# The second layer of a two-layer encoder rebuilt from half-size products in passes, with attention head by head

## The chip, the core and the metric

The kernel runs on one core of a Trainium2 chip, as one program. The metric is device microseconds from start to end; the median of three runs of the kernel before is 2737.35 us (2737.0 to 2742.38). All data is float32. Engines are named as in the profile: PE (TensorE, matmul), DVE (VectorE), ACT (ScalarE), POOL (GpSimd), and SP, the queue from which all of this kernel's transfers are issued, one after the other in the order of the program.

## The reference

2048 frames of 1024 channels go through two layers. The first is a gated mixer with its own projections; it is not changed. The second projects a shared K and V, a Q and a gate z, attends over a band of the own and eight previous chunks of 64 frames with a bias by relative position, gates, and projects out:

```python
k, v = jnp.split(rms_norm(x, g_kv) @ w_kv, 2, axis=-1)
...
q, z = jnp.split(h @ w_qz, 2, axis=-1)
...
sc = jnp.einsum('bqhd,bkhd->bhqk', qc, kc).astype(jnp.float32) + bias
sc = jnp.where(valid[None, None, None, :], sc, NEG_INF)
p = jax.nn.softmax(sc, axis=-1).astype(vc.dtype)
return jnp.einsum('bhqk,bkhd->bqhd', p, vc)
...
return (o * jax.nn.silu(z)) @ w_out
```

There are 16 heads of 64 channels. Five products of 2048 x 1024 by 1024 x 1024 make the dense work of this layer: V, K, Q, z and the output. The sum with x and a last RMS norm follow.

## The kernel before

Every float32 operand of a product is split into a high part, rounded to a format that TensorE multiplies at its full rate, and the low rest. Three matmuls (high by high, high by low, low by high; `mm3`, lines 95 to 98) stand for one. ACT writes the high part and DVE the low one.

The first layer does its six projections and its output by one level of Strassen's recursion: a product of two matrices, each cut into two by two quarters, is made of seven products of quarters (phases 1, 2, 6, 5, 7, 4, 3) in place of eight. A *pass* is one such product of 2048 x 1024 by 1024 x 1024: seven phases of eight steps, each step one PSUM tile of 128 x 512 with 12 matmuls. `run_steps` writes them in order, with operands prepared three steps ahead (`LOOK`). The left operand's combinations are split once and kept in DRAM (`hsd`, tile S); the right operand's are made from the raw weights by POOL, ACT and DVE (`make_t`, tile T).

The second layer (from 1401 us on, lines 938 ff.) does without the recursion. It goes over four blocks of 512 frames (t) and, within each, over eight pairs of heads (p). `project` makes V, Q and K of the next pair and `gate` its z (`one`, tiles pj and vp: 24 matmuls of 512 columns for a pair's K, Q or z, 24 of 256 columns for each 128 frames of V) while `score`, `flip` and `value` do the attention of the present pair. A `score` is 128 queries by up to 640 keys (tile s) with the softmax after it on DVE, ACT, DVE and POOL (lines 1062 to 1073). A `flip` transposes the probabilities on PE (tile tp, line 1093) and splits them. A `value` (tile pv, lines 1113 to 1120) multiplies two query blocks' probabilities by V. K and V of the block before come back from DRAM (`khd`, `vhd`), the scaled weights too (`wk3`, `wvv`). `share` and `take` say how many pieces of projection stand between two pieces of attention. `b4` is the output product of a block (tile bo), after the block's last head. A gain-scaled weight is loaded, multiplied on POOL and stored (`load_scaled`, lines 161 to 168) the first time.

The order of the instructions on each engine is written out by these loops; a layer below adds the semaphores, and each transfer on SP stands behind all earlier ones there.

## Time and profile before

One execution was profiled: 2736.74 us, span 2734.9 us.

| stretch (us) | what | PE busy | DVE busy | ACT busy | GB/s |
|---|---|---|---|---|---|
| 100 to 400 | first layer | 291 of 300 | 182 | 93 | 321 |
| 400 to 700 | first layer | 298 of 300 | 199 | 114 | 289 |
| 1070 to 1400 | its output product | 316 of 330 | 230 | 99 | 247 |
| 1400 to 1735 | second layer, first block | 326 of 335 | 225 | 177 | 205 |
| 1735 to 2660 | second layer, the other blocks | 922 of 925 | 731 | 561 | 150 |
| 2660 to 2735 | last block's output, end | 61 of 75 | 56 | 30 | 64 |

Matmuls overlap, so the duration of one (0.39 us for 512 columns) is longer than the distance between two starts; busy time is the time in which at least one runs. The transfer share of a window is the mean busy share of the 16 transfer engines, and a packet counts as busy from its start to its end, also while it waits.

### The profile page before, as it was taken

What the parts mean: (1) busy time and instruction counts of PE and PEld (TensorE: products, weight loads), DVE (VectorE), ACT (ScalarE), POOL (GpSimd) and SP (SyncE); (2) the same over time, 40 slices, a digit from 0 to 9 for tenths busy, and PEclk for the clock granted to TensorE, in tenths of its full rate; (3) what the DMA queues carried; (4) which work ended last, traced back from release to release, by engine and by line L of the source; (5) the groups of instructions that cost most, each with busy time, mean ns of one, the idle gap of its engine ahead of it and who ended that gap; (6) DMA issues with size and microseconds to landing.
All of it is one profiled execution on the core that took longest, in us unless ns stands there. A gap on an engine that the chain in (4) does not pass through costs nothing.

```text
span 2734.9 us, 39924 instructions
## 1 busy us (share of the span) xinstructions
PE 2667.4 (98%) x14176; PEld 2265.3 (83%) x14176; DVE 1926.6 (70%) x3211; ACT 1275.3 (47%) x2244; POOL 710.0 (26%) x767
## 2 busy tenths in 40 slices
PE   8899999999999999999999999999999999999997
PEld 6788888888778788777877888899988999889996
DVE  5655566756667667666766666877778777787777
ACT  5423243443433434222235554566655666556663
POOL 3511123241231422722024430211212212021111
PEclk9999999999999999999999999999999999999998
DMA  7799998986877869768767655545455455454432
GB/s 277 275 326 328 324 329 310 318 307 235 309 260 245 319 218 319 264 209 292 260 215 240 203 194 168 165 151 152 151 174 167 147 154 151 150 163 118 116 111 69
DMA packets 209190, 607.16 MB, mean 222 GB/s; under 512 B 24288, under 2 KB 24288, under 8 KB 208992
## 3 DMA queue, kind: packets, MB, share of 16 engines
q1 hardware_dynamic: 208992, 604.62, 66.0%
q8 instruction: 113, 1.85, 0.3%
q14 instruction: 85, 0.70, 0.1%
HBM read 466.11 MB, written 127.93 MB: 217 GB/s over the span
## 4 chain that ended last, share of the span: by engine, by line
PE 43%; DVE 7%; DMA 6%; POOL 2%; issue 1%; ACT 1%; SPq 0%; DVEq 0%; POOLq 0%; ACTq 0%
PE pj L96 5%; PE pj L97 5%; PE pj L98 5%; PE s L1054 4%; PE tp L1093 4%; PE pv L1120 4%; PE vp L98 2%; PE vp L96 2%; PE vp L97 2%; PE bo L96 2%; PE bo L98 2%; PE bo L97 2%; DMA xr<-in_x 2%; DMA A<-ytd 1%; DMA bx_b<-x1d 1%
## 5 line engine op out<-in xcount | busy, mean ns | idle before, releaser
L96 PE MATMUL P<-T,S 128*128 128x512 f32 x1248 | 496.0, 397 | 3.3 <-ACT S L255 2.1
L98 PE MATMUL P<-T,S 128*128 128x512 f32 x1248 | 490.4, 393 | 0.0
L97 PE MATMUL P<-T,S 128*128 128x512 f32 x1248 | 488.9, 392 | 0.6 <-DVE T L258 0.6
L1073 POOL TENSOR_SCALAR pr<-pr,sl 128x640 f32<-128x640 f32 (+4 forms) x256 | 198.7, 777 | 748.1 <-DVE sl L1072 662.1
L1069 ACT ACTIVATE pr<-pr,nm 128x640 f32<-128x640 f32 (+4 forms) x256 | 195.6, 764 | 270.2 <-DVE nm L1062 264.9
L96 PE MATMUL pj<-hh_b,wh_b 128*128 128x512 f32 x768 | 311.4, 406 | 0.7 <-ACT hh_b L150 0.7
L97 PE MATMUL pj<-hl_b,wh_b 128*128 128x512 f32 x768 | 302.3, 394 | 0.0
L98 PE MATMUL pj<-hh_b,wl_b 128*128 128x512 f32 x768 | 301.2, 392 | 0.0
L98 PEld LDWEIGHTS P<-T,S 128*128 128x128 f32 x1248 | 235.2, 188 | 50.0
L96 PEld LDWEIGHTS P<-T,S 128*128 128x128 f32 x1248 | 235.3, 189 | 45.7 <-ACT S L255 2.3
L97 PEld LDWEIGHTS P<-T,S 128*128 128x128 f32 x1248 | 235.6, 189 | 43.6 <-DVE T L258 1.0
L1097 DVE TENSOR_TENSOR pt<-tp,pt 128x640 fp32r<-128x640 f32 (+4 forms) x256 | 188.6, 737 | 60.2 <-ACT pt L1096 57.8
L1062 DVE CUSTOM_DVE_ANT_0 pr<-s,bias 128x640 f32<-128x640 f32 (+4 forms) x256 | 188.1, 735 | 48.7 <-PE s L1054 44.1
L98 PEld LDWEIGHTS pj<-hh_b,wl_b 128*128 128x128 f32 x768 | 144.2, 188 | 33.2
L1096 ACT CAST pt<-tp 128x640 fp32r<-128x640 f32 (+4 forms) x256 | 159.0, 621 | 22.9 <-PE tp L1093 17.8
L1093 PE MATMUL tp<-ident,pr 128*128 128x128 f32 x1120 | 164.8, 273 | 3.5 <-DVE pt L1097 2.0
L96 PEld LDWEIGHTS pj<-hh_b,wh_b 128*128 128x128 f32 x768 | 144.6, 188 | 19.6 <-ACT hh_b L150 0.9
L1093 PEld LDWEIGHTS tp<-ident,pr 128*128 128x128 f32 x1120 | 134.7, 140 | 31.4 <-issue 2.7
L97 PEld LDWEIGHTS pj<-hl_b,wh_b 128*128 128x128 f32 x768 | 145.0, 189 | 17.4
L96 PE MATMUL vp<-wh_bv,hh_b 128*128 128x256 f32 x512 | 148.3, 290 | 1.1 <-ACT hh_b L150 1.1
L98 PE MATMUL vp<-wh_bv,hl_b 128*128 128x256 f32 x512 | 145.6, 284 | 0.6 <-DVE hl_b L151 0.4
L97 PE MATMUL vp<-wl_bv,hh_b 128*128 128x256 f32 x512 | 145.1, 283 | 0.0
(216 smaller groups left out, 6054.9 us busy)
## 6 DMA issues: line engine op xcount, KB each, us to landing
S<-hsd SPq DMA_DIRECT2D x288, 512.0 KB, 5.0
rw<-in_w_a SPq DMA_DIRECT2D x108, 512.0 KB, 5.6
raw_b<-wk SPq DMA_DIRECT2D x75, 512.0 KB, 4.1
A<-ytd SPq DMA_DIRECT2D x72, 512.0 KB, 5.0
hsd<-S SPq DMA_DIRECT2D x56, 512.0 KB, 3.7
rwo<-in_w_out SPq DMA_DIRECT2D x40, 512.0 KB, 5.0
bias<-reld SPq DMA_DIRECT2D x64, 320.0 KB, 3.7
raw_bo<-in_wb_out SPq DMA_DIRECT2D x36, 512.0 KB, 3.8
```

The lines of the kernel that those rows point to most:

```text
L96: mm(ps, lh, rh, start=first, stop=False)
L97: mm(ps, lh, rl, start=False, stop=False)
L98: mm(ps, ll, rh, start=False, stop=last)
L1054: mm(ps[:, sg, :w], q[:, qb * P : (qb + 1) * P], kx[:, koff + sg * w : koff + (sg + 1) * w], start=i == 0, stop=i == 1,)
L1062: nc.vector.tensor_tensor_reduce(out=pr[:, c0:].rearrange("p (a b) -> p a b", a=nseg), in0=ps[:, :nseg, :w], in1=bias[:, c0:].rearrange("p ...
L1069: nc.scalar.activation(pr[:, c0:], pr[:, c0:], AF.Exp, scale=-1.0, bias=nm[:], accum_out=sl[:])
L1073: nc.gpsimd.tensor_scalar(pr[:, c0:], pr[:, c0:], sl[:], 1.0, op0=ALU.mult, op1=ALU.mult)
L1093: tpose(tp[:, b, :], pr[:, b * P : (b + 1) * P], ident[:])
L1096: nc.scalar.copy(oh, tp[:, b0:5, :])
L1097: nc.vector.tensor_tensor(pt[:, 1, b0 + qq : 5 + qq, cs], tp[:, b0:5, :], oh.bitcast(F32), op=ALU.subtract)
L1120: mm(po[:, 0, :], keys(i), pt[:, j, i, :], start=(t == 0 and j == 0 and i == blocks[0]), stop=(j == 1 and i == blocks[-1]),)
```

## The change

The first layer stays. The second layer's five products become passes of the recursion.

- V is a pass behind the first layer's output, on the same steps. The normalized rows are transposed and split as in the first layer's first pass, and each of the seven combinations of the rows goes to DRAM (`hs2`).
- K and Q of heads 0 to 7 are one pass behind it ("K"): the weights are now the stationary operand, and the rows' combinations come back from `hs2` in groups of four steps (`sg_load`, 2 MB each). K and Q are split and stored to DRAM (`kqd`). Beside this pass `prep_t` makes and stores the seven weight combinations of two further passes (`tbd`, 56 stores of 512 KB).
- Attention goes head by head over all 2048 frames: 256 blocks of `score` and `flip`, a `value` for each two. K, Q and V of a head are loaded from DRAM. Beside it run the two further passes (`dense`): n = 2 is K and Q of heads 8 to 15, n = 3 is z. Each is cut in two by columns, so there are four half passes, and each loads all of the rows' combinations: 56 units of 2 MB (`unit_load`), one ahead, into two buffers. `share` spreads 448 pieces of three matmuls over 250 blocks. Outputs, and z when ready, go to DRAM; `gate` loads both, multiplies on POOL and stores the product (`ogd`).
- The output is a last pass behind attention ("B"), with x added and the last norm as its steps end.

```diff
-        steps += [(n, ph, j) for n in (2, 3, 4, 5, "o") for ph in PH for j in range(NJ)]
+        steps += [(n, ph, j) for n in (2, 3, 4, 5, "o", "V", "K") for ph in PH for j in range(NJ)]
...
+        def prep_v(ph, j):
+            a11, a12 = va_[j][:, 0:512], va_[j][:, 512:1024]
+            if ph in (1, 6):
+                return s_split(ph, j, a11, "V")
+            if ph == 3:
+                tg(a12, a12, a11, op=sub)
+            if ph in (2, 3):
+                return s_split(ph, j, a12, "V")
+            return s_load(ph, j, "V")
...
+        def sg_load(ph, g):
+            i = len(sgs)
+            pool, tag, bufs = (kqp[0], "Sg", 2) if i % 3 else (sh, "hh", 1)
+            t = pool.tile([P, 4, 2, 4, P], F32R, tag=tag, name=f"Sg{i}", bufs=bufs)
+            nc.sync.dma_start(
+                t[:].rearrange("p j a k c -> p j a (k c)").bitcast(F32),
+                hs2[ph, g][:],
+            )
+            sgs[ph, g] = t
...
+        def product_k(ps, t, w):
+            o = ps[:].rearrange("p (a b) -> p a b", a=4)
+            for k in range(4):
+                mm3(o, w[k][0], w[k][1], t[:, :, 0, k, :], t[:, :, 1, k, :], k == 0, k == 3)
...
+            def put(ph, v):
+                hi, lo = (
+                    ca.tile([P, 1024], F32R, tag="S", name=f"wt{n}{q}_{ph}{i}", bufs=6)[:]
+                    for i in range(2)
+                )
+                split(hi, lo, v)
+                for i, t in enumerate((hi, lo)):
+                    nc.sync.dma_start(tbd[n, ph][:, i, q, :], t.bitcast(F32))
...
+        for u in range(4):
+            for i, f_ in enumerate(prep_t(2 + u // 2, u % 2)):
+                at(nk + 3 + 13 * u + 2 * i, f_)
...
+            def load_k(h):
+                t = kt[h] = sb.tile([P, S], F32R, tag="K", name=f"K{h}", bufs=2)
+                for i in range(2):
+                    nc.sync.dma_start(
+                        t[i * 64 : i * 64 + 64].bitcast(F32),
+                        kqd[0][h // 2][i, h % 2 * 64 : h % 2 * 64 + 64, :],
+                    )
...
+            units = [
+                (n, cq, ph, g) for n, cq in ((2, 0), (2, 1), (3, 0), (3, 1)) for ph in PH
+                for g in range(2)
+            ]
...
+            def unit_load(i):
+                if i >= len(units):
+                    return
+                n, cq, ph, g = units[i]
+                if g == 0:
+                    cs = slice(cq * 256, cq * 256 + 256)
+                    for hl in range(2):
+                        w = wq[n, cq, ph, hl] = sh.tile(
+                            [P, 2, 2, 256], F32R, tag="T", name=f"w{n}{cq}_{ph}_{hl}", bufs=8
                         )
+                        nc.sync.dma_start(
+                            w[:].bitcast(F32),
+                            tbd[n, ph][:, hl].rearrange("p q (k c) -> p q k c", k=2)[:, :, :, cs],
+                        )
+                t = sgq[i] = sh.tile(
+                    [P, 4, 2, 4, P], F32R, tag=("hl", "hh")[i % 2], name=f"Sq{i}"
+                )
+                nc.sync.dma_start(
+                    t[:].rearrange("p j a k c -> p j a (k c)").bitcast(F32), hs2[ph, g][:]
+                )
...
+            def dense():
+                base = 10000
+                unit_load(0)
+                for i, (n, cq, ph, g) in enumerate(units):
+                    unit_load(i + 1)
+                    for ct in range(2):
+                        flush(base + 2 * i + ct)
+                        ps = pmm.tile([P, 512], F32, tag="mm", name=f"Pb{n}{cq}_{ph}_{g}{ct}")
+                        o = ps[:].rearrange("p (a b) -> p a b", a=4)
+                        t = sgq[i]
+                        for k in range(4):
+                            w = [
+                                wq[n, cq, ph, hl][:, k // 2, k % 2, ct * P : ct * P + P]
+                                for hl in range(2)
+                            ]
+                            mm3(o, *w, t[:, :, 0, k, :], t[:, :, 1, k, :], k == 0, k == 3)
+                            yield
+                        evict(10 * n + cq, ph, 2 * g + ct, ps, done_b(n, cq))
+                flush(1 << 20)
...
+                first = max(0, 4 - 2 * g)
+                full = range(max(first, 1), 5)
+                seq = [(i, slice(0, 256)) for i in full]
+                if first == 0:
+                    seq.append((0, slice(0, P)))
+                seq.append((5, slice(P, 256)))
+                for n, (i, cs) in enumerate(seq):
+                    for j in range(2):
+                        mm(
+                            po[:, g % 2, cs], keys(i), pt[:, j, i, cs],
+                            start=g % 2 == 0 and n == 0 and j == 0,
+                            stop=g % 2 == 1 and n == len(seq) - 1 and j == 1,
                         )
...
+            def gate(p, t):
+                v = sh.tile([P, 2, 512], F32, tag="raw", name=f"og{p}_{t}", bufs=4)
+                cs = slice(t * 512, t * 512 + 512)
+                nc.sync.dma_start(v[:, 0], od[p][:, cs])
+                nc.sync.dma_start(v[:, 1], zd[p][:, cs])
+                nc.gpsimd.tensor_tensor(v[:, 0], v[:, 0], v[:, 1], op=ALU.mult)
+                nc.sync.dma_start(
+                    ogd[p // 4, t][:, :, p % 4, :], v[:, 0].rearrange("p (a b) -> p a b", a=4)
+                )
...
+            def one_gate():
+                for i, x_ in enumerate(gates):
+                    if x_ in zready:
+                        gate(*gates.pop(i))
+                        return
...
+            def share(b):
+                return 224 * min(1.0, (b + 1) / 116) + 224 * max(0.0, min(1.0, (b - 115) / 134))
...
+                if b + 2 < NB2:
+                    score(b + 2)
+                take(share(b - 0.5))
+                flip(b)
+                if b % 2 == 0 and b:
+                    value(b // 2 - 1)
+                take(share(b))
+                one_gate()
+            value(NB2 // 2 - 1)
...
+            steps = [("B", ph, j) for ph in PH for j in range(NJ)]
```

Three places show what moves. Names carry t, pair or head, and block; a name with w30 is the weight of the third pass's first half, Sq a group of rows.

PE beside attention, before (block 2, pair 5): six matmuls of a projection stand between a score and a flip.

```order
L1054 MATMUL s2_5_3_20479<-K2_2_1_19968,Qh2_2_1_19865 128x320 x2
L1054 MATMUL s2_5_3_20479<-K2_2_1_19968,Ql2_2_1_19866 128x320 x2
L96 MATMUL pj2_2_2_20442<-hh_b2_18434,wh_b2_2_2_20438 128x512
L97 MATMUL pj2_2_2_20442<-hl_b2_18435,wh_b2_2_2_20438 128x512
L98 MATMUL pj2_2_2_20442<-hh_b2_18434,wl_b2_2_2_20439 128x512
L96 MATMUL pj2_2_2_20442<-hh_b2_18434,wh_b2_2_2_20438 128x512
L97 MATMUL pj2_2_2_20442<-hl_b2_18435,wh_b2_2_2_20438 128x512
L98 MATMUL pj2_2_2_20442<-hh_b2_18434,wl_b2_2_2_20439 128x512
L1093 MATMUL tp2_5_1_20497<-ident_128,pr2_5_1_20387 128x128 x5
L96 MATMUL pj2_2_2_20442<-hh_b2_18434,wh_b2_2_2_20438 128x512
```

And after, in head 9:

```order
L1225 MATMUL tp9_3_20406<-ident_80,pr9_3_20343 128x128 x4
L84 MATMUL Pb30_5_01_20402<-Sq34_20158,w30_5_0_20154 128x512
L85 MATMUL Pb30_5_01_20402<-Sq34_20158,w30_5_0_20154 128x512
L86 MATMUL Pb30_5_01_20402<-Sq34_20158,w30_5_1_20156 128x512
L1188 MATMUL s9_6_20419<-K9_20007,Q9_1_20295 128x320 x4
L84 MATMUL Pb30_5_01_20402<-Sq34_20158,w30_5_0_20154 128x512
L85 MATMUL Pb30_5_01_20402<-Sq34_20158,w30_5_0_20154 128x512
L86 MATMUL Pb30_5_01_20402<-Sq34_20158,w30_5_1_20156 128x512
L1225 MATMUL tp9_4_20435<-ident_80,pr9_4_20366 128x128 x5
L1256 MATMUL pv9_0_20380<-pt9_2_20373,V4_0_19403 128x256 x6
L1256 MATMUL pv9_0_20380<-pt9_2_20373,V4_0_19403 128x128 x2
```

The pieces are of three matmuls now, with fewer of them per score, and the moving operand Sq and the weight w30 are both fresh from DRAM.

SP where K of a pair is projected, before:

```order
L995 DMA Qh2_2_0_19859<-Qh2_2_0_19859 64x512 [waits DMAHW2_49,Activation_49]
L995 DMA Ql2_2_0_19860<-Ql2_2_0_19860 64x512 [waits DMAHW3_49,DVE_49]
L995 DMA Qh2_2_1_19865<-Qh2_2_1_19865 64x512 [waits DMAHW4_49,Activation_49]
L161 DMA raw_b2_4_1_20620<-wk3_4_68 128x1024 [waits DMAHW5_49,DVE_49]
L995 DMA Ql2_2_1_19866<-Ql2_2_1_19866 64x512 [waits DMAHW6_49,DVE_49]
L1009 DMA K2_2_1_19968<-khd1_2_86 128x512 [waits DMAHW7_49]
L1007 DMA khd2_2_94<-K2_2_0_19963 128x512 [waits DMAHW0_49,DVE_49]
L1009 DMA K2_3_0_20426<-khd1_3_87 128x512 [waits DMAHW1_49,PE_49]
L161 DMA raw_b2_4_0_20721<-wk3_4_68 128x1024 [waits DMAHW2_49,DVE_49]
L1007 DMA khd2_2_94<-K2_2_1_19968 128x512 [waits DMAHW3_49,DVE_49]
```

And where K is a pass, after:

```order
L920 DMA Sg2_13610<-hs2_2_0_231 128x4096 [waits DMAHW3_49]
L203 DMA rwK_6_011_13638<-in_w_b 128x1024 [waits DMAHW4_49,DVE_49]
L203 DMA rwK_6_001_13640<-in_w_b 128x1024 [waits DMAHW5_49,DMAHW0_49,Pool_49]
L203 DMA rwK_6_111_13642<-in_w_b 128x1024 [waits DMAHW6_49,DMAHW1_49,Activation_49]
L990 DMA tbd2_1_291<-wt20_10_13644 128x1024 [waits DMAHW7_49,Activation_49]
L990 DMA tbd2_1_291<-wt20_11_13645 128x1024 [waits DVE_49]
L990 DMA tbd2_2_292<-wt20_20_13694 128x1024 [waits Activation_49]
L990 DMA tbd2_2_292<-wt20_21_13695 128x1024 [waits DMAHW2_49,DVE_49]
L990 DMA tbd2_3_293<-wt20_30_13700 128x1024 [waits DMAHW3_49,Activation_49]
L990 DMA tbd2_3_293<-wt20_31_13701 128x1024 [waits DMAHW4_49,DVE_49]
L951 DMA kd0_243<-kq0_0_0_13708 128x512 [waits DMAHW5_49,Activation_49]
L951 DMA kd0_243<-cK_0_13682 128x512 [waits DMAHW6_49,DVE_49]
```

In place of half a megabyte of weights, and K and V rows of 256 KB, stand groups of rows of 2 MB (Sg, shape 128x4096), raw weights and stores of weight combinations (tbd); each store waits for ACT or DVE.

SP beside attention, before, with the next pair's weights and the V of the block before:

```order
L1031 DMA bias2_5_20166<-reld5_117 128x640 [waits DMAHW4_49,DVE_49]
L967 DMA vhd2_1_109<-V2_1_0_20042 128x512 [waits DMAHW5_49,DVE_49]
L967 DMA vhd2_1_109<-V2_1_1_20093 128x512 [waits DMAHW6_49,DVE_49]
L967 DMA vhd2_1_109<-V2_1_2_20160 128x512 [waits DMAHW7_49,DVE_49]
L161 DMA raw_bv2_2_0_20831<-wvv2_74 128x1024 [waits DMAHW0_49,DVE_49]
L967 DMA vhd2_1_109<-V2_1_3_20215 128x512 [waits DMAHW1_49,DVE_49]
L975 DMA Vh2_2_0_20823<-vhd1_2_106 128x512 [waits DMAHW2_49,PE_49]
L975 DMA Vh2_2_1_20825<-vhd1_2_106 128x512 [waits DMAHW3_49,PE_49]
```

And after, where the first gate is made (og0):

```order
L1117 DMA w30_6_0_19781<-tbd3_6_303 128x4x256 [waits DMAHW5_49]
L1117 DMA w30_6_1_19783<-tbd3_6_303 128x4x256 [waits DMAHW6_49]
L1124 DMA Sq32_19785<-hs2_6_0_239 128x4096 [waits DMAHW7_49,PE_49]
L1146 DMA zd0_14893<-c30_0_19694 128x512 [waits DMAHW0_49]
L1281 DMA og0_0_19809<-od0_14885 128x512 [waits DMAHW1_49]
L1077 DMA Q8_2_19836<-qd4_255 64x2x512 [waits DMAHW2_49]
L1282 DMA og0_0_19809<-zd0_14893 128x512 [waits DMAHW3_49,DMAHW0_49]
L1077 DMA Q8_2_19836<-qd4_255 64x2x512 [waits DMAHW4_49]
L1084 DMA V4_2_19839<-vsd1_8_283 128x256 [waits DMAHW5_49]
L1084 DMA V4_2_19839<-vsd1_9_284 128x256 [waits DMAHW6_49]
L1284 DMA ogd0_0_14901<-og0_0_19809 512x1x128 [waits DMAHW7_49,Pool_49]
L1084 DMA V4_2_19839<-vsd1_10_285 128x256
```

The gate's two loads and its store stand with four other loads among them, and the store waits for POOL; the next group of rows (Sq32) and its weights stand ahead.

981 lines of the change are left out of this document (469 added, 512 removed).

## The prediction

> **What bounds the kernel now.** I read the busy shares and the 40 slices of the page first, then the window of the second layer, then the order in time of TensorE's work there, then the rows on transfers.
>
> ```profile
> PE 2667.4 (98%) x14176; PEld 2265.3 (83%) x14176; DVE 1926.6 (70%) x3211; ACT 1275.3 (47%) x2244; POOL 710.0 (26%) x767
> ...
> DMA  7799998986877869768767655545455455454432
> GB/s 277 275 326 328 324 329 310 318 307 235 309 260 245 319 218 319 264 209 292 260 215 240 203 194 168 165 151 152 151 174 167 147 154 151 150 163 118 116 111 69
> DMA packets 209190, 607.16 MB, mean 222 GB/s; under 512 B 24288, under 2 KB 24288, under 8 KB 208992
> ```
> ```profile
> 1401.00:2735.00 1334.00, 1307.87 (x7874) 1156.23 (x7872) 1011.41 (x2046) 767.41 (x1444) 302.01 (x471) 0.99 0.51 159
> ```
>
> TensorE is busy all the time. In the second layer (from 1401 us, the window row: length, busy time of PE, PEld, DVE, ACT, POOL, clock, DMA share, GB/s) it is busy for 1308 of 1334 us, while transfers run at 159 GB/s, half of what the first layer moves (the slices fall from 329 to about 150). So the second layer is bound by TensorE and has transfers to spare. The change trades one for the other.
>
> What one matmul costs is the distance between starts, since they overlap:
>
> ```profile
> 1703.11 0.39 PE L98 MATMUL bo<-wh_bo,ol 128*128 128x512 f32 x1
> ...
> 1705.38 0.39 PE L96 MATMUL bo<-wh_bo,oh 128*128 128x512 f32 x1
> ```
> ```profile
> 2002.26 0.46 PE L1054 MATMUL s<-K,Qh 128*128 128x320 f32 x2
> 2002.55 0.46 PE L1054 MATMUL s<-K,Ql 128*128 128x320 f32 x2
> 2002.85 0.28 PE L96 MATMUL vp<-wh_bv,hh_b 128*128 128x256 f32 x1
> ...
> 2003.08 0.28 PE L98 MATMUL vp<-wh_bv,hl_b 128*128 128x256 f32 x1
> 2003.20 0.28 PE L96 MATMUL vp<-wh_bv,hh_b 128*128 128x256 f32 x1
> ...
> 2003.56 0.40 PE L96 MATMUL pj<-hh_b,wh_b 128*128 128x512 f32 x1
> 2003.80 0.40 PE L97 MATMUL pj<-hl_b,wh_b 128*128 128x512 f32 x1
> 2004.03 0.39 PE L98 MATMUL pj<-hh_b,wl_b 128*128 128x512 f32 x1
> 2004.26 0.71 PE L1093 MATMUL tp<-ident,pr 128*128 128x128 f32 x5
> 2004.72 0.36 PE L1113 MATMUL pv<-pt,Vh 128*128 128x256 f32 x1
> ...
> 2006.00 0.40 PE L96 MATMUL pj<-hh_b,wh_b 128*128 128x512 f32 x1
> ```
>
> The ten intervals from 1703.11 to 1705.38 give 0.227 us for 512 columns, 0.23 between attention work. 256 columns take 0.12 us, one block's scores 0.59, its five flips 0.46, one pair's values 1.28. The count for the second layer before: pj 2304 x 0.23 = 530, vp 1536 x 0.12 = 184, bo 768 x 0.227 = 174, flips 1120 x 0.092 = 103, scores 192 x 0.59 and 64 of the first four blocks of a head at some 0.35 (by their columns) = 136, values 96 x 1.28 and 32 short ones at 0.7 (six matmuls) = 145, transposes 128 x 0.11 (eight in 0.87) = 14. Sum 1286 of 1334; 48 are waits, 18 of them the tail from the last matmul to 2734.9, as two rows of the chain that ended last show:
>
> ```profile
> 1393.88 0.87 PE tr_b L145 x8
> ...
> 2716.72 0.24 PE bo L98
> ```
>
> **What it takes from TensorE.** Seven products of half size replace eight. Dense work is then five passes (V; K and Q of half the heads; K and Q of the rest; gates; output) of 672 matmuls of 512 columns. Per stage: V 672 x 0.227 and 224 transposes x 0.11 = 177; K 152; attention with the two passes beside it 1344 x 0.23 = 309, flips 103, scores 136, values 149 (eight matmuls of 256 columns and four of 128 per pair; the narrow ones I put between 0.06 and 0.12 us, half and all of the 256-column price, so 1.2 to 1.44, taken 1.32); output 152. Sum 1179, so 107 us less.
>
> **What it adds in transfers.** Counted in units of 512 KB from the new code. V: weights 18, rows 16, the split rows stored 56 and read back 24, V out 32: 146. K: weights 18, 14 groups of split rows at 4 units = 56, weight combinations for the later passes 16 read and 56 stored, K and Q out 32: 178. Attention: split rows 56 x 4 = 224 (each of the four half passes reads all of them again), combined weights 56, K 32, Q 64, V 32, bias 10, outputs and gates to DRAM and back 80, K and Q of the second pass 32: 530. Output: 91. In all 945 units, 495 MB, against 159 GB/s x 1334 us = 212 MB before. The price of a unit is bounded by the fastest stretches of this trace:
>
> ```profile
> 450.00:460.00 10.00, 10.00 (x50) 7.99 (x49) 5.38 (x7) 2.95 (x5) 0.00 (x0) 1.00 1.03 416
> 360.00:400.00 40.00, 38.54 (x180) 31.45 (x179) 23.53 (x32) 17.66 (x28) 14.68 (x11) 1.00 0.96 348
> 440.00:500.00 60.00, 60.00 (x278) 48.96 (x277) 40.63 (x51) 19.23 (x31) 16.54 (x11) 1.00 0.97 332
> 450.00:550.00 100.00, 98.16 (x469) 80.11 (x468) 69.20 (x92) 38.55 (x61) 16.69 (x13) 1.00 0.96 326
> ```
>
> Over 10 us 416 GB/s (1.26 us a unit), over 40 us 348, over 100 us 326 (1.61). The long stretches are held back by demand too, TensorE being busy throughout, and the new stages queue more than the engines can take, so I go above the middle: 380 GB/s, 1.38 us a unit. Then V needs 201 us of transfers against 177 of TensorE, K 246 against 152, attention 731 against 697, output 126 against 152. Three of the four stages turn from TensorE to transfers, and K is the clearest: nothing there covers the 94 us, since each group of rows is loaded only three steps (2.7 us each) ahead, behind the stores of weights and results on the one queue.
>
> **The queue.** Each of 32 gates loads two tiles, multiplies on POOL and stores, in order on SP. The trace has that pattern in 32 scaled weights:
>
> ```profile
> SPq L168 <- DMA raw_b<-in_w_kqz: 44.7, 17, 4.0
> SPq L168 <- POOL raw_b L165: 40.5, 21, 3.0
> ...
> SPq L168 <- POOL raw_bv L165: 14.3, 7, 2.3
> SPq L168 <- DMA raw_bv<-in_w_vv: 7.5, 6, 2.9
> ```
>
> SP stood for 107 us on these, 3.3 a store. Hidden then, behind spare transfers; now it lies in the half of attention that needs most of them. Between nothing and 107; other loads stand between a gate's loads and its store, so I take 50.
>
> **The joins.** The output pass needs the last head's gated output, which goes through DRAM twice before the first product, and its weights queue behind that store:
>
> ```profile
> 2688.17 0.59 ACT ot L1132
> 2688.78 0.70 DVE ot L1134
> ```
> ```profile
> hsd<-S SPq DMA_DIRECT2D x56, 512.0 KB, 3.7
> ```
>
> Copy and add 1.3, store, load and store again with POOL between, then weights at 3.7 a transfer and their split: 18 us (10 to 25). V's start follows the first layer as the projections did; the tail after the last product stays 18.
>
> **Vector engines.** In attention VectorE has 256 blocks at 0.735 and 0.737 us, and some 220 us of reciprocals, evictions, splits and gates: about 600 of 697. No bound by itself.
>
> ```profile
> L1097 DVE TENSOR_TENSOR pt<-tp,pt 128x640 fp32r<-128x640 f32 (+4 forms) x256 | 188.6, 737 | 60.2 <-ACT pt L1096 57.8
> L1062 DVE CUSTOM_DVE_ANT_0 pr<-s,bias 128x640 f32<-128x640 f32 (+4 forms) x256 | 188.1, 735 | 48.7 <-PE s L1054 44.1
> ```
>
> **The sum.** V 201 + K 246 + attention 731 + 50 + output 152 with 2% of waits, 156 + join 18 + tail 18 = 1420, where 1334 stood. On the profiled span of 2734.9: 2821. That execution took 2736.7 us, 1.8 around the span, and the median of the runs shown, 2737.35, is 0.6 above it; with these 2.4 the forecast is 2824 us, 3% slower.
>
> **The rivals.** (a) Transfers keep up: 416 GB/s all the way, gates hidden. V 184, K 224, attention at TensorE's 697, output 156, 36 for join and tail: 1297, so 2700, faster. It decides at one number: the whole stands level at 1.28 us a unit with the 50 us of the gates (410 GB/s), at 1.34 without (392). Only 10 us stretches were that fast, but none had so deep a queue. (b) TensorE stays the bound, transfers hidden: 1179 + 30 of waits + 36 = 1245, so 2648. K would need 178 units in 152 us, 612 GB/s; no row comes near. (c) A cap: what the trace holds for 40 us, 348 GB/s, is all that the engines give in a stage that always has transfers queued, and the 10 us stretch was a burst. A unit is 1.507 us: V 220, K 268, attention 799 and 50, 156, 36: 1529, so 2932. For it speaks that the transfer share is 0.96 or 0.97 in all three long rows; against it that a share over 0.96 goes with 416 GB/s as well, so a long share may count packets that only wait. [...]
>
> **How the numbers follow.** The forecast (2745 to 2890) gets 0.52, (c) and what lies around it, 2890 to 3000, 0.23, beyond 0.03 (the gates' full 107 and a dry queue on top), (a) 0.15, (b) 0.03, level 0.04. A difference under 0.2% (5 us) can't be told from none here. That is 0.19 faster, 0.04 same, 0.77 slower. The range goes from (a)'s 2700 to 2960, (c) with half of the gates' other 57; what it leaves out, (b), all beyond 2960 and a little below 2700, is about 0.2.
>
> **What would show it.** Right: K takes about 246 us with a transfer share near 1 and TensorE waiting on loads of Sg at every fourth step; attention shows PE waiting on Sq, more in its second half; SP waits on POOL at the gate's store. Wrong: a rate of 400 GB/s or more held over hundreds of us, which brings (a). Waits over some 4 us could also halve the clock as here, where the matmuls behind an idle stretch take 0.43 us each; K at half clock would take 14 x 48 x 0.43 = 289.
>
> ```profile
> 1386.97 0.43 PE Po L96
> 1387.40 0.43 PE Po L97
> ```

## The result: 16% slower, and where the time went

The changed kernel takes 3176.25 us (median of four runs, 3165.43 to 3189.63), the kernel before 2737.18 beside it: 1.1605 times as long, with a 95% interval of 1.1556 to 1.1654. The forecast was 3% slower with a range that ended at 2960; the direction was right, the size far too small. The profiled execution took 3165.43 us with a span of 3163.6.

The page of the changed kernel, busy shares and the 40 slices:

```profile
PE 2766.8 (87%) x13216; PEld 2244.3 (71%) x13216; DVE 1865.8 (59%) x2973; ACT 1219.4 (39%) x2110; POOL 895.8 (28%) x807
...
PEclk9999999999999999989998879999999988798897
DMA  7898989777686976758899998888967888877864
GB/s 280 310 326 317 339 306 317 292 251 288 238 318 238 314 248 223 278 205 339 331 347 376 356 355 262 276 288 273 284 209 242 279 253 250 265 236 219 276 204 164
DMA packets 314834, 883.40 MB, mean 279 GB/s; under 512 B 32272, under 2 KB 93712, under 8 KB 303632
```

The second layer, stage by stage (length, busy time of PE, PEld, DVE, ACT, POOL, clock, DMA share, GB/s): V; K; attention with the side passes; join and output; tail.

```profile
1399.00:1610.00 211.00, 187.19 (x888) 150.98 (x888) 123.02 (x182) 85.07 (x143) 58.02 (x49) 0.96 0.86 322
1610.00:1874.00 264.00, 175.82 (x672) 138.52 (x672) 118.93 (x128) 104.83 (x145) 76.46 (x50) 0.84 0.96 360
1874.00:2933.00 1059.00, 874.47 (x4702) 713.03 (x4702) 541.21 (x1247) 447.52 (x911) 252.25 (x332) 0.90 0.83 258
2933.00:3147.00 214.00, 170.72 (x677) 133.54 (x675) 164.59 (x246) 53.59 (x79) 94.81 (x70) 0.90 0.67 220
3147.00:3163.00 16.00, 0.42 (x1) 0.00 (x0) 10.81 (x26) 0.00 (x0) 3.80 (x6) 0.61 0.44 164
```

| stage | forecast us | measured us |
|---|---|---|
| V | 201 | 211 |
| K, first to last product | 246 | 246 |
| last K product to first scores | none | 18 |
| attention, first scores to last values | 731 + 50 | 1059 |
| join | 18 | 16 |
| output products | 156 | 198 |
| tail | 18 | 16 |
| sum | 1420 | 1764 |

K came out to the microsecond, with a share of 0.96 and TensorE waiting for Sg as forecast (engine, line, releaser: us, times, longest):

```profile
PE Pk L84 <- DMA Sg<-hs: 74.6, 10, 13.0
```

Of the 344 us that are missing, attention has 278. TensorE is no longer full there (874 of 1059, the clock at 0.90 after 1.00 in the same stage before), and the transfers are not quite full either (0.83).

What ended TensorE's, the other engines' and SyncE's waits in attention (read as the line above):

```profile
ACT pt L1228 <- PE tp L1225: 263.2, 202, 7.7
DVE pt L1229 <- ACT pt L1228: 205.8, 180, 4.6
POOL og L1283 <- DMA og<-zd: 82.3, 22, 12.1
PE tp L1225 <- DVE pt L1229: 68.0, 76, 2.4
...
PE s L1188 <- DMA Q<-qd: 21.2, 5, 17.8
PE Pb L84 <- DMA Sq<-hs: 17.1, 4, 6.7
```
```profile
SPq L1269 <- DVE o L1268: 228.1, 30, 17.6
SPq L1284 <- POOL og L1283: 108.6, 29, 8.1
```

TensorE's longest waits in sum stand at the flips (68 us here for their buffer), not at Sq (17). A stretch of TensorE's work in order of time tells why: two flips of five blocks stand one behind the other, with nothing between them, and the first four blocks of the second wait 2.39 us for the one transpose buffer.

```profile
2102.25 0.39 PE L86 MATMUL Pb<-Sq,w 128*128 128x512 f32 x1
2102.48 0.72 PE L1225 MATMUL tp<-ident,pr 128*128 128x128 f32 x5
2105.58 0.63 PE L1225 MATMUL tp<-ident,pr 128*128 128x128 f32 x4 [2.39 <-DVE pt L1229]
2105.97 0.48 PE L84 MATMUL Pb<-Sq,w 128*128 128x512 f32 x1
```

The chain that ended last shows four in a row at another place (start, us, work), 2.5 us each where the forecast counted 0.46:

```profile
2048.23 0.78 PE tp L1225 x5
2049.04 0.04 issue
2049.08 0.70 ACT pt L1228
2049.81 0.84 DVE pt L1229
2050.65 0.14 issue
2050.78 0.75 PE tp L1225 x5
2051.53 0.02 issue
2051.56 0.70 ACT pt L1228
2052.28 0.84 DVE pt L1229
2053.11 0.14 issue
2053.25 0.75 PE tp L1225 x5
...
2055.77 1.21 PE tp L1225 x5
```

In TensorE's program order, 122 of the 255 pairs of successive flips have less than 1.5 us of other matmuls between them and 47 less than 0.3; in the kernel before no pair has less than 1.5. In the changed kernel this order is not the one in which its loops are written: the layer below that adds the semaphores also schedules. The order stands in the program, so this could have been read before the run.

The transfers of K (246 us) and of attention (1059 us), queue by queue: packets, MB, share of the 16 engines' time.

```profile
q1 hardware_dynamic: 23192, 89.75, 95.4%
```
```profile
q1 hardware_dynamic: 119949, 272.65, 82.4%
```

In K 90 MB kept the 16 engines full for 235 us, 382 GB/s, the forecast's 380. In attention 273 MB took 873 us of all engines, 312 GB/s: 1.68 us for 512 KB that moved, not 1.38. With the few transfers outside this queue it is 876 us, 1.65 for each of the 530 units that the forecast counted.

### The profile page after: what moved, and what is told of

Read it like the earlier page. It is cut to its first block, busy times and chain, and to the rows that moved or that the text cites. A ratio compares the mean times of both kernels' runs of the same rounds, so it can differ in the third digit from the quotient of the medians.

```text
span 3163.6 us, 38540 instructions
## 1 busy us (share of the span) xinstructions
PE 2766.8 (87%) x13216; PEld 2244.3 (71%) x13216; DVE 1865.8 (59%) x2973; ACT 1219.4 (39%) x2110; POOL 895.8 (28%) x807
## 4 chain that ended last, share of the span: by engine, by line
PE 28%; DMA 14%; DVE 10%; ACT 5%; issue 4%; POOL 4%; SPq 1%; DVEq 0%; POOLq 0%; ACTq 0%
PE tp L1225 4%; PE pv L1256 3%; PE Pb L84 3%; PE Pb L85 3%; PE Pb L86 3%; PE s L1188 3%; DVE pt L1229 2%; ACT pt L1228 2%; DMA Sg<-hs 2%; DVE pr L1196 2%; DMA og<-zd 1%; PE Po L86 1%; PE Po L85 1%; PE Po L84 1%; PE Pv L84 1%
## 5 line engine op out<-in xcount | busy, mean ns | idle before, releaser
L1207 POOL TENSOR_SCALAR pr<-pr,sl 128x640 f32<-128x640 f32 (+4 forms) x256 | 190.0, 742 | 671.9 <-DVE sl L1206 575.5
L1225 PE MATMUL tp<-ident,pr 128*128 128x128 f32 x1120 | 193.5, 302 | 99.3 <-DVE pt L1229 68.0
L1256 PE MATMUL pv<-pt,V 128*128 128x256 f32 (+1 forms) x1344 | 226.6, 308 | 32.6 <-ACT pt L1228 28.1
L1188 PE MATMUL s<-K,Q 128*128 128x320 f32 (+4 forms) x896 | 196.1, 336 | 52.9 <-DVE nm L1196 29.5
L1256 PEld LDWEIGHTS pv<-pt,V 128*128 128x128 f32 x1344 | 199.7, 213 | 59.3 <-ACT pt L1228 44.6
L84 PE MATMUL Pb<-Sq,w 128*128 128x512 f32 x448 | 198.6, 443 | 17.1 <-DMA Sq<-hs 17.1
L1188 PEld LDWEIGHTS s<-K,Q 128*128 128x128 f32 x896 | 145.0, 195 | 95.8 <-DVE nm L1196 64.6
L85 PE MATMUL Pb<-Sq,w 128*128 128x512 f32 x448 | 187.8, 419 | 0.0
L86 PE MATMUL Pb<-Sq,w 128*128 128x512 f32 x448 | 186.6, 417 | 0.0
L84 PE MATMUL Pk<-Sg,TK 128*128 128x512 f32 x224 | 96.8, 432 | 76.1 <-DMA Sg<-hs 74.6
L291 DVE TENSOR_TENSOR x<-P,x 128x512 f32<-128x512 f32 x144 | 97.9, 683 | 45.5 <-PE P L86 45.5
```

The source lines that it names most:

```text
L84: mm(ps, lh, rh, start=first, stop=False)
L85: mm(ps, lh, rl, start=False, stop=False)
L86: mm(ps, ll, rh, start=False, stop=last)
L291: last["evict"] = nc.vector.tensor_tensor(*args, **kw).ins.name
L1188: mm(ps[:, sg, :w], qt[h, qb // 4][:, i, qb % 4 * P : qb % 4 * P + P], kx[:, k0 * P + sg * w : k0 * P + (sg + 1) * w], start=i == 0, stop= ...
L1207: nc.gpsimd.tensor_scalar(pr[:, c0:], pr[:, c0:], sl[:], 0.5, op0=ALU.mult, op1=ALU.mult)
```

## The experiments

The theories that the expectations name. ORDER: the flips' clumps are the cause. TRANSFERS, later RATE: the engines' own time for the bytes. QUEUE: SyncE stands at a wait and the loads behind it come late. CHAIN (called LATENCY at first): the loop from scores over VectorE, ScalarE and GpSimd to flip and value is too long, whatever the transfers do. PARTITIONS: transfers that fill only 64 of 128 partitions are slow; SPREAD: a small outermost count leaves engines idle. GATE: GpSimd waits for a gate's tiles with the probabilities behind it. TENSORE: the rest is its own work. All times are of the attention stage from the first scores to the last values, 1059 us in the changed kernel, unless they are of the whole; "engines" is the time for which its packets would keep all 16 DMA engines busy. Some expectations count in the 15 to 18 us ahead of the first scores (1075, 1021, 957 and 873 for what is 1059, 1003, 942 and 855 here). Each edit ran once unless said; the four runs of the changed kernel lie 24 us apart, so a difference of the whole below that is not told from none. The stage alone repeats better: two runs of the fastest version have 855 and 852.

| run | whole us | attention us | engines us |
|---|---|---|---|
| changed kernel | 3176 | 1059 | 876 |
| order held | 3140 | 1014 | 877 |
| two flip buffers | 3165 | 1047 | 887 |
| order, two flip buffers | 3126 | 1003 | 880 |
| order, no reads of Sq | 2975 | 855 | 558 |
| order, two buffers, no Sq, no preparation in K | 2887 | 846 | 552 |
| order, two buffers, late stores | 3065 | 942 | 873 |
| the same, runs of 4 KB | 3064 | 948 | 857 |
| order, two buffers, loads from ScalarE | 3146 | 1010 | 859 |
| late stores, full width, outer count 2 | 3778 | 1626 | 826 |
| late stores, no Sq | 2975 | 845 | 556 |
| late stores alone | 3150 | 1037 | 884 |
| order, no Sq, gates last | 2968 | 846 | 561 |
| late stores, full width, interleaved | 2972 | 855 | 776 |
| the same, GpSimd held | 2972 | 849 | 776 |
| the same, SyncE held too | 3035 | 905 | 772 |
| interleaved reads alone | 3031 | 927 | 790 |
| attention alone | 2792 | 682 | 389 |
| fastest version, measured again | 2973 | 852 | 776 |

From the late stores on, rows without "alone" have the order held and two flip buffers too, but for "gates last", which has one; the fastest version is the interleaved one.

### The order on TensorE, the flip buffers, Sq

The order is held by a dependency of each matmul on the one written before it, without a semaphore:

```diff
-    mm, tpose = nc.tensor.matmul, nc.tensor.transpose
+    mm, tpose = pe(nc.tensor.matmul), pe(nc.tensor.transpose)
```

> The only edit: in the attention stage every TensorE instruction is put behind the one written before it, so TensorE works the scores, flips, values and dense matmuls in the order in which the kernel writes them (about six dense matmuls a block, three on either side of a flip). In the changed kernel 122 of 255 pairs of flips in a row have less than 1.5 us of other matmuls between them, 47 less than 0.3 us; here 45 and 1. Theory ORDER (TensorE waits because flips stand back to back and each then waits out the chain through the one transpose buffer): the 131 us of waits ahead of flips fall under 50, the 66 us at the lower clock go with them in part; the stage of 1059 us becomes 850 to 920 us, the time 2970 to 3040 us. Theory TRANSFERS (the reloaded Sq, Q and gate tiles arrive too late, and the order only follows them): the waits move from the flips to the dense matmuls, the stage stays at 1020 to 1120 us, the time at 3130 to 3240 us. Theory LATENCY (the loop from scores over VectorE, ScalarE and GpSimd to flip and value is longer than the matmuls between them, in any order): the stage stays at 1000 to 1060 us, the time at 3120 to 3180 us, waits on scores, flips and values as before.

45 us less of attention, 36 of the whole; with the order held the first scores come 29 us after K's last product, not 18, and that takes 11 back. The flips' waits halved (131 to 64 us, worked out from the distances between TensorE's starts), but 162 us of waits appeared at the scores, most of it for Q:

```profile
PE s L85 <- DMA Q<-qd: 130.3, 27, 11.7
PE tp L85 <- DVE pt L1248: 43.1, 61, 2.2
```

Made to wait in order, TensorE waits for the tiles. So the clumps look like the scheduler's way around late tiles, and ORDER is a small part.

```diff
-    pmm = bufs=4, ptr = bufs=1        # the attention stage alone
+    pmm = bufs=2, ptr = bufs=2
```

> The only edit: in the attention stage the flips have two PSUM buffers in place of one, and the matmul results two in place of four (PSUM is full); the order on TensorE is not held. Theory ORDER: two flips in a row no longer wait for one another, but 137 of 255 pairs stand closer than 1.5 us and the third of a clump still waits; the stage of 1059 us falls to 930 to 1000 us, the time to 3050 to 3120 us. Theory TRANSFERS: no change, 3140 to 3200 us. Theory LATENCY: a gain only if the transpose buffer is the loop's tight place, 3000 to 3100 us; none, 3140 to 3200 us, if it is the scores' buffer.

> Both edits together: TensorE in the written order in the attention stage, and two transpose buffers with two result buffers. Theory ORDER: with the written order one buffer is nearly enough, so this is within 40 us of the run with the order alone, 2940 to 3040 us. Theory LATENCY: the stage falls by 100 us or more against the run with the order alone. Theory TRANSFERS: 3130 to 3240 us, as with the order alone.

12 and 11 us of the stage, and of the whole nothing that the spread lets one tell (3165 alone): the second flip buffer is worth little. What two result buffers in place of four cost the dense matmuls shows in the run without Sq and preparation below (48 us of waits).

```diff
+                if i > 1:
+                    sgq[i] = sgq[i % 2]
+                    return
                 t = sgq[i] = sh.tile(...)
```

> TensorE in the written order in the attention stage, and the Sq tiles of the side passes are loaded twice only, the first two of 56; all later units multiply by these two (so Q's second half and the gates of the second layer come from the wrong passes, and 113 MB of reads are left out). Theory TRANSFERS: all of the stage's loss was in these reads; against the run with the order alone the stage falls by 200 us or more, to 780 to 850 us, the time to 2880 to 2960 us. Theory ORDER: at most 40 us under the run with the order alone. Theory LATENCY: equal to the run with the order alone within 20 us.

159 us less than with the order alone: TRANSFERS were the largest part so far, but the stage stopped at 855, with 0.65 of the transfers' time used, where TensorE's own work is 700. 108 us of waits ahead of flips were left (from the distances again), and the clock rose from 0.91 to 0.98:

```profile
1890.00:2904.00 1014.00, 801.43 (x4692) 686.96 (x4691) 544.85 (x1247) 444.85 (x912) 251.16 (x332) 0.91 0.86 265
```
```profile
1883.00:2738.00 855.00, 760.27 (x4694) 650.53 (x4693) 541.28 (x1247) 445.13 (x912) 251.35 (x332) 0.98 0.65 182
```

### K's preparation, and two flip buffers without Sq

```diff
-        for u in range(4):
-            for i, f_ in enumerate(prep_t(2 + u // 2, u % 2)):
-                at(nk + 3 + 13 * u + 2 * i, f_)
```

> On top of the written order and the two transpose buffers (the run of 3126 us, attention stage 1021 us, K stage 275 us): Sq is loaded twice only, as in the run with one transpose buffer, and the weight combinations of the later passes are neither made nor stored in the K stage; attention loads the same bytes from other tiles in their place (Q's second half and the gates are wrong, and 72 transfers of 512 KB are left out in K). Attention: theory CHAIN (the 108 us of waits ahead of flips that were left without Sq come from the one transpose buffer) says these waits fall under 30 and the stage from 873 to about 790 us; if they come from late probabilities (GpSimd, or the scores before it), the waits stay and the stage with them, 850 to 880. K stage: theory RATE (transfers bound it: 178 units at 1.38 us) says 106 units are left, 146 us, under TensorE's 152, so 170 to 190 us with the 18 us before the first scores; if something else bounds it, 250 or more.

K's products took 170 us in place of 246, and TensorE's waits for Sg fell from 75 to 14: the preparation for the later passes costs 76 us there. With the share of 0.95 this fits a stage bound by its transfers; the edit also took away the preparation's work on the other engines, which was not tried by itself. In attention the flips' waits fell from 108 to 42 us, most of what CHAIN gave the one buffer, and nearly all of the 42 that are left wait for GpSimd's probabilities. But the stage fell only from 855 to 846, since 48 us of waits on dense matmuls' buffers and 35 on values came in their place.

### Late stores

```diff
-                nc.sync.dma_start(od[p][...], o[:])
+                pend.append((cur[0] + 1, put))
...
-                nc.gpsimd.tensor_tensor(v[:, 0], v[:, 0], v[:, 1], op=ALU.mult)
-                nc.sync.dma_start(ogd[p // 4, t][...], ...)
+                pend.append((cur[0] + 3, mult))
```

> On top of the run of 3126 us: the heads' output is stored one block later than written before, a gate's loads come three blocks after the stores that they read, its multiplication three blocks behind its loads and its store two blocks behind that, so that SyncE finds each done. Theory QUEUE (SyncE stands at these waits, 109 us at the gates' stores, 117 at the gates' reads, 228 at the heads' outputs, and the loads of Q and Sq behind them come late): waits of the scores on Q fall from 130-150 us under 70, the transfers' share rises from 0.87 to 0.93 or more, the stage falls from 1021 to 930 to 970 us, the time to 3035 to 3080 us. Theory RATE (the engines are full with small packets as it is): under 25 us gained, 3100 to 3130 us. Theory CHAIN: no change, 3115 to 3135 us.

61 us of the stage, as QUEUE said; SyncE's wait at the gates' stores is 26 us where the changed kernel had 109, the scores' on Q 78 (a little over what was expected), and the transfers' share rose to 0.93. From here the engines' 873 us fill most of the stage's 942:

```profile
1895.00:2836.00 941.00, 794.20 (x4688) 686.12 (x4687) 544.43 (x1247) 444.00 (x912) 252.72 (x331) 0.94 0.93 285
```

> The late stores alone on the changed kernel: one transpose buffer, order on TensorE left free. Theory QUEUE (SyncE's waits are the cause, and the clumps of flips follow from late Sq): the stage falls from 1075 to 980 to 1020 us, the time to 3075 to 3115 us. Theory ORDER (the clumps in TensorE's order hold the stage by themselves): the clumps stay and so does most of the time, 3130 to 3170 us.

Alone, on the free order, they are worth 22 us of the stage and 26 of the whole, about the spread: the clumps stay, as ORDER said.

> On top of the run of 3126 us: Q, K, V and bias are loaded from ScalarE's queue in place of SyncE's, all else as there. Theory QUEUE (the small loads stand behind 2 MB of Sq and behind SyncE's waits on the one queue): the scores' waits on Q, 130 to 150 us, fall under 40, the stage falls from 1021 to 900 to 950 us, the time to 3005 to 3055 us; what Q gains Sq may lose, then TensorE waits on Sq in its place. Theory RATE: the waits move from Q to Sq and the stage stays at 990 to 1030 us. Theory CHAIN: the stage stays, and waits on flips and values take the place of those on Q.

With Q, K, V and bias on ScalarE's queue the waits on Q went (12.7 us at scores), and came back at dense matmuls (87), values (86) and flips (76). The stage stayed, as RATE and CHAIN both said, but not with the waits on Sq that RATE named (under 4 us): they stand on flips and values, as CHAIN had it. Most of the flips' waits are for GpSimd's probabilities, and GpSimd waited 142 us for the gates' z, where the changed kernel had 82.

### Why the bytes take so long

```diff
-                            tbd[n, ph][:, hl].rearrange(...)[:, :, :, cs],
+                            tbd[n, ph][:, hl, cq].rearrange(...),
```

> On top of the late stores: the combined weights and V are read as runs of 4 KB in place of 1 KB, the same bytes into the same tiles, V in one transfer in place of four (the data are wrong, they come from the wrong columns). In the changed kernel 43,600 packets of 1 KB take 57 ns each (286 GB/s over 16 engines, 156 us of all engines), packets of 4 KB in the K stage 166 ns (396 GB/s). Theory RATE: the same 44.7 MB take 113 us, 43 us less of transfer time, and the stage falls by 30 to 45 us against the run with late stores alone. Theory QUEUE: 93 transfers fewer to issue, under 15 us. Theory CHAIN: none.

Nothing (1 us of the whole). The runs of 4 KB took 224 ns where four of 1 KB had taken 240, and the same length took 166 in K. The length of the runs was not the cause.

```diff
-                for i in range(2):
-                    nc.sync.dma_start(t[i * 64 : i * 64 + 64], kqd[0][h // 2][i, rows, :])
+                nc.sync.dma_start(t[:], kqd[0][h // 2][:, rows, :])
...
-                    nc.sync.dma_start(q[i * 64 : i * 64 + 64], src.rearrange("a p c -> p a c"))
+                    nc.sync.dma_start(q[:, i], src[i].partition_broadcast(2))
```

> On top of the late stores (3065 us, attention stage 957 us of which the 16 engines are full for 871): K and Q are read by transfers that fill all 128 partitions, two of 256 KB each for Q and one of 1 MB for K, in place of two that fill 64 partitions each; bytes, run lengths and tiles stay. In the changed kernel K's runs of 8 KB take 580 ns (225 GB/s over 16 engines) where an 8 KB run elsewhere takes 309, and Q's runs of 2 KB 117 ns where stores of 2 KB take 86. Theory PARTITIONS (a transfer into half of the partitions moves at little more than half the rate): K's 71 us of transfer time become about 40, Q's 115 about 85, the stage falls by 40 to 65 us. Theory RATE with any other cause of the slow packets: under 15 us.

Both at once: the packets became as fast as PARTITIONS said (K 344 ns), and the whole kernel took 713 us longer. The engines were half idle. Two windows of this kernel, and SyncE's issues in the second of them:

```profile
2280.00:2290.00 10.00, 9.48 (x54) 8.20 (x53) 5.62 (x12) 4.12 (x8) 0.81 (x1) 0.86 0.96 244
2292.00:2308.00 16.00, 3.17 (x14) 2.59 (x14) 1.58 (x4) 1.45 (x3) 2.63 (x5) 0.64 0.13 54
```
```profile
2290.66 17.39 SPq L1099 DMA_DIRECT2D Q<-qd  x2
```

For 16 us the share is 0.13, two engines of sixteen: by the packets' times exactly 2.0 are in flight. These transfers have an outermost count of 2 (two halves of 64 rows), and only two engines work on them, while SyncE stands at the two issues of Q for 17.39 us. That the count sets the number of engines is my reading of this; counts between 2 and the 64 of the next run were not tried.

So the two halves were interleaved over the partitions, which makes the outermost count 64; K's and Q's rows are permuted alike:

```diff
+                    kqd[0][h // 2][:, rows, :].rearrange("i p c -> p i c"),
...
+                        src[i].partition_broadcast(2).rearrange("i p c -> p i c"),
```

> On top of the late stores (3065 us, stage 957): K and Q are read into all 128 partitions, as in the run that took 3778 us, but with the halves of a head interleaved over the partitions, so that the outer count of a transfer is 64 and not 2 (K's and Q's rows are permuted alike, the scores are the same sums). In that run the stretches in which K or Q moved held just two packets in flight, 2.0 of 16 engines for 18 us in a row. Theory SPREAD (the outermost count sets over how many engines a transfer is spread): here all 16 work, packets of K take some 345 ns in place of 597, the engines' time falls from 871 to 820 to 835 us, and the stage from 957 to 900 to 935 us, the time to 3010 to 3045 us. If the full width itself is what jams the queue: 3500 us or more again.

93 us less than with the late stores alone, about twice what was expected, since some of the other packets gained as well. Mean ns of a packet in the attention stage, worked out from the packets' records:

```
                       late stores   outer count 2   interleaved
K, 8 KB                    597            344            364
Q, gates, K/Q out, 2 KB    111             98            100
weights, V, 1 KB            60             54             50
bias, 2.5 KB               185            146            108
Sq, 16 KB                  697            795            694
```

```profile
1884.00:2740.00 856.00, 776.00 (x4695) 669.66 (x4693) 542.68 (x1247) 443.66 (x913) 252.96 (x332) 0.97 0.91 314
```

K's transfers into 64 partitions ran at 220 to 225 GB/s over the 16 engines (597 ns for 8 KB here, 581 in the changed kernel), interleaved over all 128 at 360 (364 ns), and the shorter runs of the table took less time beside it; Sq's runs of 16 KB stayed (697 and 694 ns). Why half of the partitions gives that rate was not shown.

> The interleaved reads of K and Q alone on the changed kernel: nothing held, no late stores, one transpose buffer. Theory PARTITIONS (reads into half of the partitions are the largest single cause): the engines' time falls from 876 to some 780 us, Sq and Q come earlier, and the stage falls from 1075 to 950 to 1000 us, the time to 3050 to 3100 us. Theory QUEUE or ORDER as the main cause: under 40 us gained, 3135 us or more.

Alone on the changed kernel the interleaved reads gain 132 us in attention and 146 of the whole, more than all other edits together. The clumps became fewer too (70 pairs under 1.5 us for 122), so part of this gain is the order; with the order held the same edit is worth the 87 us from 942 to 855.

### What is left without transfers

> On top of the late stores: Sq is loaded twice only (113 MB of reads left out, so Q's second half and the gates are wrong). It tells what the stage is worth with neither the transfers' rate nor the gates' waits. Theory RATE (after the late stores the stage is bound by the engines' 871 us): the stage falls from 957 to 770 to 810 us, near TensorE's 700 and waits of some 70. Theory CHAIN (scores, flips and values run into one another with 2.8 us of matmuls a block): 840 to 870 us, as without Sq but with the gates' waits (864), and then some 140 us of waits on TensorE are the engines' own.

845 us, in the range of CHAIN: neither the reads of Sq nor the gates' stores hold this stage. The gates are not out of it, though: GpSimd still waited 120 us for their tiles, and flips 34 us for probabilities.

> On top of the written order on TensorE with Sq loaded twice only (attention 873 us, one transpose buffer): all 32 gates are done after the last head's values, none beside attention (Q's second half and the gates are wrong as there). Theory GATE (GpSimd stands at a gate's multiplication until its tiles have landed, 82 to 102 us, and the probabilities of the next blocks stand behind it, so the flips come late): the waits ahead of flips fall from 108 to under 40 us and the time from the first scores to the last values from some 855 to 770 to 800 us; the gates then come on top at the end, 40 to 90 us. Theory CHAIN (the loop over four engines itself is too long for 2.8 us of matmuls a block): first scores to last values stays at 830 to 860 us, and flips keep waiting for the transpose buffer.

The flips' waits stayed at 100 us and the stage at 846. The scheduler drew the gates back: 31 of the 32 multiplications start before the last values, though later than before and closer together, so the run does not test what was meant. GpSimd's waits for the gates' tiles did fall from 133 to 53 us, with 9 us gained, which speaks against GATE as a large part.

```diff
-            gen = dense()
+            gen = iter(())
```

> Attention by itself: on the run with the order held and one transpose buffer, the side passes are left out altogether, with their reads of Sq and weights (the second half of the heads takes K and Q of the first, the gates multiply the output by itself). TensorE's own work is then some 390 us. Theory CHAIN (scores, VectorE, ScalarE, GpSimd, flip, ScalarE, VectorE, value with single buffers for scores and flips): the stage takes 680 to 850 us, 2.7 to 3.3 us a block, nearly what it takes with the side passes and without Sq (873), so the side passes fill gaps and the chain sets the time. Theory TENSORE: 400 to 500 us, and the 140 us of waits that were left come from the side passes' own results.

682 us, 2.66 us a block, with the order held and one flip buffer, for some 390 us of TensorE's work. A stretch of it in order of time, one block:

```profile
2201.59 0.74 PE L85 MATMUL tp<-ident,pr 128*128 128x128 f32 x5 [0.41 <-DVE pt L1248]
...
2202.42 0.69 ACT L1247 CAST pt<-tp 128x640 fp32r<-128x640 f32 x1 [1.02 <-PE tp L85]
...
2203.15 0.82 DVE L1248 TENSOR_TENSOR pt<-tp,pt 128x640 fp32r<-128x640 f32 x1 [0.89 <-ACT pt L1247]
...
2204.15 0.71 PE L85 MATMUL tp<-ident,pr 128*128 128x128 f32 x5
```

From one flip to the next 2.56 us: flip, copy on ScalarE, subtraction on VectorE, and the buffer is free. Attention alone goes at nearly the pace of this loop. That it is the only one is not shown: TensorE waited 42 us for this buffer, 39 for VectorE's reciprocals and 55 for the scores' buffer. The side passes then add 173 us (855 less 682, both with one flip buffer) of their 309: they fill some of the gaps, not all. The expectation that attention alone would take nearly as long as with them was wrong. What exactly holds the 845 is open; with one flip buffer the waits stand at flips, with two at dense matmuls, values and flips that wait for GpSimd.

### Queues held in the written order, and the fastest version

> On top of the interleaved reads: GpSimd works probabilities and gates in the written order, a gate's multiplication at least three blocks behind its loads and never ahead of a block's probabilities that were written before it. Theory GATE: GpSimd's waits on a gate's tiles (31 us left with the late stores) go under 10, and the stage falls by 10 to 40 us against the run before this one. Theory RATE: under 10 us.

> On top of that: SyncE issues the attention stage's transfers in the written order too (with the late stores), in place of the order that the scheduler chose. Theory QUEUE (SyncE's remaining waits, 121 us at the heads' outputs and 84 at Sq's buffer, still delay the loads behind them): the transfers' share rises to 0.95 or more and the stage falls by 20 to 60 us against the run before it. If the scheduler's order was the better one, loads that stand behind Sq's wait for its buffer come late, and the stage grows by 20 us or more.

GpSimd in the written order: TensorE's waits for probabilities went to 2 us and the stage gained 6, next to nothing, so here GATE is small. SyncE in the written order: 63 us slower; a load of Sq then waits for its buffer with Q's loads behind it (SyncE waited 121 us for TensorE, 85 for an earlier Sq to land). The scheduler's order was the better one.

> The fastest correct version so far once more, with an interval: order held on TensorE, two transpose buffers, late stores, interleaved reads of K and Q. All theories: 2965 to 2980 us, 1.085 to 1.09 times the kernel before; it does not come near it, since attention stays at 855 to 870 us where TensorE has 700 us of work and the other four stages are as in the changed kernel.

2972.74 us (four runs, 2967.77 to 2982.2), 1.0882 times the kernel before (1.0853 to 1.0910). No version came near it. What the edits took off the changed kernel's attention, one on the other: order 45, second flip buffer 11, late stores 61, interleaved reads 87; together 204 of 1059.

## Why the prediction was wrong

Two steps failed, both in the term "attention 731 + 50", which took 1059. Of the 278 us that are missing there, 145 are the price of a unit (876 for 731), and 133 the rule that the larger of two totals is the time of the stage (183 between 876 and 1059, less the 50 put down for the gates).

- **Which resource.** Right for K: it came to 246 us as worked out, 178 units at 1.38, and without the 72 units of preparation to 170. The exact hit is in part luck: 171 units moved in that time, in 235 us of full engines, and 11 us were not full. V took 211 for 201. In attention neither TensorE nor the transfers were full.
- **The price of a unit: the first step that failed.** "So I go above the middle: 380 GB/s, 1.38 us a unit" was one price for every shape. It held where transfers fill 128 partitions (382 GB/s in K). Attention's K, Q and output tiles are loaded and stored over 64 partitions, and there a counted unit cost 1.65: 876 us, not 731. With full-width reads it was 1.46. The trace of before had a warning: its copies of Q's halves (128 KB each, 64 partitions, from one half of SBUF to the other and not from DRAM) took 141 ns for a run of 2 KB, mean of the 25 copies with nothing else in flight, where most runs of 2 KB beside attention took 80 to 100. The stretches that I priced by hold none of that width.
- **"Attention 731 against 697": the second step that failed.** I took the larger of two totals as the time. But 697 was TensorE's work, not what the stage takes: without Sq's reads it took 845 to 855, and attention alone 682. So even at 1.38 a unit the stage would not have come down to 731. A flip's loop of 2.5 us, less the flip's own 0.46, needs some 2.1 us of other matmuls to hide it. In the kernel before 3.3 us stood there (median; mean 4.2); the change leaves 2.1 to 2.2 on average and a median of 1.6, with no margin. That the flip went on costing 0.46 us was the silent assumption. The transfers at 876 and the chain at about 850 are then nearly equal, and the stage took 183 us more than the engines; how the two add up is not shown in detail.
- **The gates.** SyncE stood at their stores for 108.6 us, next to the upper bound of 107. Storing late, heads' outputs too, was worth 61 us with the order held, beside 50 forecast, and 22 on the free order. GpSimd's waits for the gates' tiles, 82 us ahead of the probabilities, I had not priced. The late stores took them to 31, and how much of the 61 us was theirs is not separated; of what remained, holding GpSimd's order gained 6.
- **Joins.** The output's join took 16 us for 18. The like one ahead of attention, where K and Q go through DRAM, takes 18 and was not in the sum. The tail took 16 for 18.
- **Output.** 198 us for 156. VectorE is busy for three quarters of it, TensorE waits 28 us, 21 of them on the split of rows, and the clock is 0.90. Only read from the trace, not tried.
- **Rivals.** (a) and (b), on the faster side, were far off. (c), the cap of 348 GB/s, was the nearest at 2932, for a wrong reason: K moved 365 GB/s over its whole 246 us, and 382 over the 235 us for which its packets fill the engines.
- **Slips in the working.** They change no term. The terms of the sum give 2823, not 2824. With the gates' 50 us the level point is 1.22 us a unit (430 GB/s), not 1.28, since by the forecast's own rule attention can't go under its 697. The chances named add up to 0.18 faster and 0.78 slower, not 0.19 and 0.77.
- **What would show it.** K's waits on Sg and SyncE's on GpSimd came as said; in attention TensorE waited for Sq only 17 us; with the order held the waits stood on Q, which comes over the same queue. The clock fell as feared: 66 of attention's 1059 us are matmuls stretched at the lower clock, and the stage's clock of 0.90 was 0.97 in the interleaved version. The 4 us named for it are no threshold that the traces show: in the trace of before, starts 0.43 us apart follow waits of 3.12, 3.69 and 3.95 us alike.

## What to carry to other kernels

Price a transfer by the trace's packets of the same shape, width in partitions ahead of all: one rate for all bytes was off by a fifth here. Where matmuls are taken away from beside a loop over several engines, compare what is left per turn with what the loop needs to be hidden, and look in the program order whether the turns still have work between them. Where two limits come out nearly equal, forecast more than the larger: here 1059 us from 876 and about 850.

## What the runs showed of the hardware

- K's and Q's transfers into half of the partitions slowed those beside them as well: with both at full width (interleaved), runs of 1 KB into all partitions went from 60 to 50 ns and of 2.5 KB from 185 to 108, while runs of 16 KB stayed (697 and 694).
- K's and Q's transfers with an outermost count of 2 kept two of the 16 engines busy (share 0.13), SyncE stood 17.39 us at two issues of Q, and the kernel took 713 us longer.
- Runs of 1 KB and of 4 KB moved at nearly the same rate in attention (274 and 293 GB/s).
- In the trace of before, TensorE's highest rate is that of matmuls of rounded operands (0.227 us for 512 columns, 0.44 ns a column); no faster format was run, so that this is its full rate is not shown.
